# A hybrid attention and state-space layer: ten panels of the input projection with their channels in rows, a new panel order, and other groupings in the state-space part

## The chip, the cores and the metric

The kernel runs on one core of a Trainium2 chip. The metric is the device time of one execution in microseconds. Three runs of the kernel before took 601.91 to 602.18 us, their median 602.09 us.

## What is computed

One layer of a decoder over 256 tokens of width 1024, in float32. One combined input projection feeds an attention mixer and a Mamba-2 mixer that run side by side; their gated sum, a SwiGLU feed-forward block and a gated embedding term follow.

```python
h = rms_norm(x, ln1_g)                       # 256 x 1024
q, k, v, z, xbc, dt_raw, gate_a, gate_b = split(h @ w_in)
qh, kh = rms_norm per head of q, k           # 16 heads of 64
y_a = causal_attention(qh, kh, v) @ w_o_attn # one block of 256 tokens
xbc = silu(causal_depthwise_conv(xbc, conv_w, conv_b))   # 3072 channels, 4 taps
xs, bm, cm = split(xbc)                      # 2048, 4 groups x 128, 4 groups x 128
dt = softplus(dt_raw + dt_bias); a = -exp(a_log) * dt    # 32 heads
# two chunks of 128 tokens; per group of 8 heads:
y = ((cm @ bm.T) * exp(segsum(a))) @ (xs * dt)           # inside a chunk
y += exp(cumsum(a)) * (cm @ state of the chunk before)   # carried state
y = (y + d_skip * xs) * silu(z)
y_b = rms_norm(y, per group of 512, ssm_norm_g) @ w_o_ssm
x += (sigmoid(gate_a) * y_a + sigmoid(gate_b) * y_b) @ w_out
x += (silu(g) * u) @ w_down                  # g, u = rms_norm(x, ln2_g) @ w_gate_up
x += (p @ w_ple_proj) * sigmoid(rms_norm(x, ln3_g) @ w_ple_gate)
```

## The kernel before

**Products in three parts.** Every weight and every activation is split into two float32r numbers, a high one and the rest, and a product a·w is formed as ah·wh + ah·wl + al·wh (`Panel.step`, L355). A chunk of 4 x 128 rows by 512 columns of weights comes in two loads of 512 KB on SyncE's queue into a `raw` tile; `split_w` (L260) makes `wh` by a cast on ScalarE (its line in the trace is L151, the helper `act`) and `wl` by a subtraction on VectorE (L263). `w_tiles` (L255) holds 4 `raw`, 3 `wh` and 6 `wl` tiles of [128, 2, 512]. The activations `h_act` are the transposed inputs times the gain, split, without the row's 1/rms; the 1/rms (`rstd1`, from `x_stats`, L389) comes in when a result leaves PSUM.

**Panels.** `PANELS` (L34) lists the blocks of 512 columns of the input projection in the order of the work; `yb` stands for a block of the state-space output projection. A `Panel` (L333) takes two `psg` banks (tile `g`, four in all), one for each 128 tokens: the activations of 128 tokens are the stationary side, 512 columns of weights move, so the tokens come to stand in the rows. Eight blocks of 128 rows, two token halves and three parts are 48 products of 512 columns. The main loop (L903 to L910) goes through the list, opens a panel, runs its products and starts its evacuation.

**Evacuation.** q and k (`evac_qk`, L556) are normed on VectorE, with a power on GpSimd for each token half, then transposed. v and the gates `ga`, `gb` leave by a copy or a Tanh on ScalarE. xbc (`evac_xbc`, L499) and z (`evac_z`, L533) need their channels in the rows: two evacuations with the scale rstd1 on ScalarE into `s2` tiles, four groups of transposes on TensorE (L192) into `psb` banks (tile `pb`, four), two groups for each half of the panel, then for xbc a ScalarE multiplication by the last tap and three shifted multiply-adds on VectorE (L520), and a SiLU by Tanh.

**The state-space part.** `dt_task` (L416) forms dt by 16 products of 256 columns, then a chain of small operations, and `e0`, `e1`, the decays to the end and from the start of a chunk. `ssm_task` (L608) goes through four groups of eight heads, each in two runs of four heads (`units`, L716). Of a group, `prep` (L645) transposes xs and multiplies it by dt; of a run, `decay_rows` (L628) fills rows on GpSimd and by two small loads, `seg` (L669) forms the decay by a product and an Exp and multiplies it with the scores (L676), `out_` (L681) makes eight products with 64 stationary columns, two at a time on the two halves of the array (`halves`). `off` (L697) adds the carried state: one float32 product of 512 columns, a multiplication by e1 with heads in the columns (L705), four transposes and an addition (L713). `ssm_finish` (L734) multiplies with z and splits the result for the output projection.

**What sets the order.** TensorE runs one list: the panel products are chained in program order, and between two of them the `Filler` (L78) puts products of side tasks. It keeps a clock of its own, `fill.now`, which each product moves on; a task yields the time from which it may go on, which is the present time plus a number of `LAG` (L68). So `LAG` and the ranks of the tasks decide after which panel product a transpose or a score stands. ScalarE and VectorE work through their lists in order too; there the compiler's scheduler sets the order by four priorities (`w` for weight splits, `ev` for evacuations, `bg` for side tasks, `mm`), of which `w` goes first. Tiles come from pools, so that a new tile waits until the last reader of the one in its place is done.

## Time and profile before

| | |
|---|---|
| median of three runs | 602.09 us |
| the profiled execution: span from its first to its last instruction | 600.7 us |
| TensorE busy (matmuls) | 593.9 us, 99%, 2965 instructions |
| weight loads into TensorE | 484.6 us, 81% |
| VectorE busy | 424.1 us, 71% |
| ScalarE busy | 338.6 us, 56% |
| GpSimd busy | 38.7 us, 6% |
| mean granted TensorE clock | 1.000 |
| moved by DMA | 103.88 MB, 173 GB/s |

The profile is of one execution. A matmul's record runs longer than its share of the engine's time, because matmuls overlap in the pipeline: the 1508 records of products from `wh` have a mean of 395 ns, while their starts lie some 227 ns apart. What a product costs is therefore read from the distance of starts in the timeline, or from a stretch of the chain divided by its count. In rows of the trace `g` is a bank of a panel, `pb` a bank of a side task, `s` any working tile.

### The profile page before, as it was taken

Reading aid. Unit: us, or ns where it says so; the run is one execution under the profiler, and the core shown is the slowest. Engines: PE = TensorE matmul, PEld = TensorE weight load, DVE = VectorE, ACT = ScalarE, POOL = GpSimd, SP = SyncE. Lnnn points to the kernel's source line nnn. Section 1 sums busy time; section 2 is a strip of 40 time slices with the busy share of each in tenths; the row PEclk is TensorE's granted clock in tenths of the full one; section 3 lists DMA queues with packets and bytes.
Section 4 is the critical chain, followed back from the end, with each engine's and each line's share of the span. In section 5 each row is a group of like instructions: output and inputs, shape, how many; then the busy total and the mean of one; then the engine's idle time right before and its main releaser. Section 6 shows DMA issues by size and latency. Waiting matters only on the chain.

```text
span 600.7 us, 8147 instructions
## 1 busy us (share of the span) xinstructions
PE 593.9 (99%) x2965; PEld 484.6 (81%) x2965; DVE 424.1 (71%) x668; ACT 338.6 (56%) x513; POOL 38.7 (6%) x47
## 2 busy tenths in 40 slices
PE   8999999999999999999999999999999999999997
PEld 7888888787777878887787788888888888888886
DVE  5689999978997765677875475756756666646465
ACT  6766666556775545576646444755544544445353
POOL 2000103412010011101000000000000000000000
PEclk9999999999999999999999999999999999999999
DMA  8945644533444445555544475556565555555641
GB/s 278 323 152 175 210 142 142 174 131 117 140 127 149 143 150 170 187 166 160 162 161 164 139 232 188 185 165 208 163 200 188 161 201 187 190 188 182 201 141 70
DMA packets 31192, 103.88 MB, mean 173 GB/s; under 512 B 3568, under 2 KB 4912, under 8 KB 31152
## 3 DMA queue, kind: packets, MB, share of 16 engines
q1 hardware_dynamic: 31152, 103.36, 53.3%
q8 instruction: 23, 0.38, 0.3%
q14 instruction: 17, 0.14, 0.1%
HBM read 102.23 MB, written 1.05 MB: 172 GB/s over the span
## 4 chain that ended last, share of the span: by engine, by line
PE 96%; DVE 1%; DMA 1%; ACT 0%; SPq 0%; issue 0%; ACTq 0%
PE g L170 85%; PE pb L170 6%; PE pb L192 5%; DMA raw<-in_head 1%; SPq L248 0%; DVE s L750 0%; ACT wh L151 0%; DVE s L658 0%; ACT s L151 0%; DVE wl L263 0%; DVE s L785 0%; DVE s L663 0%; DVE s L742 0%; DVE s L1063 0%; DVE s L1064 0%
## 5 line engine op out<-in xcount | busy, mean ns | idle before, releaser
L170 PE MATMUL g<-wh,s 128*128 128x512 f32 (+1 forms) x1508 | 486.7, 395 | 0.6 <-ACT wh L151 0.6
L170 PEld LDWEIGHTS g<-wh,s 128*128 128x128 f32 x1508 | 282.7, 189 | 59.6 <-issue 1.8
L263 DVE TENSOR_TENSOR wl<-raw,wh 128x1024 fp32r<-128x1024 f32 (+2 forms) x193 | 230.4, 1196 | 129.6 <-ACT wh L151 127.0
L151 ACT ACTIVATE wh<-raw 128x1024 fp32r<-128x1024 f32 (+2 forms) x193 | 199.9, 1038 | 177.7 <-PE g L170 149.8
L170 PE MATMUL g<-wl,s 128*128 128x512 f32 (+1 forms) x754 | 294.2, 392 | 0.0
L170 PEld LDWEIGHTS g<-wl,s 128*128 128x128 f32 x754 | 142.1, 189 | 27.8 <-issue 1.0
L151 ACT ACTIVATE s<-pb 128x512 f32<-128x512 f32 (+4 forms) x64 | 33.6, 544 | 30.4 <-PE pb L192 16.1
L192 PEld LDWEIGHTS pb<-ident,s 128*128 128x128 f32 x302 | 37.9, 140 | 11.4 <-issue 0.9
L192 PE MATMUL pb<-ident,s 128*128 128x128 f32 x302 | 47.1, 272 | 0.0
L151 ACT ACTIVATE s<-g,rstd 128x512 f32<-128x512 f32 (+1 forms) x50 | 28.5, 583 | 20.5 <-PE g L170 18.7
L520 DVE SCALAR_TENSOR_TENSOR s<-pb,vecs,s 128x255 f32<-128x255 f32 (+2 forms) x72 | 32.0, 475 | 1.4 <-ACT s L151 1.2
L170 PE MATMUL pb<-s,s 128*64 128x128 f32 (+6 forms) x328 | 32.6, 304 | 0.4 <-ACT s L151 0.4
L151 ACT ACTIVATE s<-pb,vecs 128x256 f32<-128x256 f32 (+2 forms) x48 | 25.9, 550 | 11.1 <-PE pb L192 5.0
L170 PEld LDWEIGHTS pb<-s,s 128*64 128x64 f32 (+2 forms) x328 | 23.1, 154 | 9.9 <-issue 4.7
L381 POOL TENSOR_TENSOR rstd<-tiny,mhalf 128x2 f32<-128x2 f32 x3 | 2.3, 762 | 315.2 <-DVE tiny L380 295.3
L151 ACT ACTIVATE s<-s 128x512 f32<-128x512 f32 (+3 forms) x24 | 19.0, 792 | 4.3 <-DVE s L978 4.0
L571 POOL TENSOR_TENSOR tiny<-tiny,mhalf 128x8 f32<-128x8 f32 x8 | 16.0, 1995 | 73.2 <-DVE tiny L569 73.2
L635 POOL TENSOR_SCALAR_AFFINE_SELECT rr<-a_h 128x512 fp32r<-128x512 f32 x16 | 13.6, 860 | 100.2 <-PE pb L170 61.7
L151 ACT ACTIVATE s<-s,tiny 128x128 f32<-128x128 f32 (+1 forms) x32 | 14.2, 444 | 6.5 <-DVE tiny L788 6.5
L1022 DVE SCALAR_TENSOR_TENSOR s<-g,rstd,s 128x256 f32<-128x256 f32 x22 | 10.6, 481 | 7.5 <-ACT s L151 7.5
L676 DVE TENSOR_TENSOR s<-s,s 128x512 f32<-128x512 f32 x16 | 11.9, 748 | 0.3 <-ACT s L151 0.3
L1023 DVE SCALAR_TENSOR_TENSOR s<-g,rstd,s 128x256 f32<-128x256 f32 x22 | 10.7, 484 | 0.7
(120 smaller groups left out, 235.2 us busy)
## 6 DMA issues: line engine op xcount, KB each, us to landing
raw<-in_w_big SPq DMA_DIRECT2D x176, 512.0 KB
raw<-in_head SPq DMA_DIRECT2D x4, 512.0 KB
s<-in_xk SPq DMA_DIRECT2D x4, 512.0 KB
raw<-in_head SPq DMA_DIRECT2D x7, 256.0 KB
raw<-in_w_pp SPq DMA_DIRECT2D x2, 512.0 KB
raw<-in_w_dn SPq DMA_DIRECT2D x2, 512.0 KB
out<-s SPq DMA_DIRECT2D x3, 256.0 KB
xraw<-in_head SPq DMA_DIRECT2D x2, 256.0 KB
```

Of the source, the lines that this page charges most:

```text
L151: return nc.scalar.activation(o, i, f, **kw)
L170: ins = nc.tensor.matmul(o, lhsT, rhs, start=start, stop=stop).ins
L192: queue(nc.tensor.transpose(o, i, ident[: i.shape[0], : i.shape[0]]).ins, False)
L263: nc.vector.tensor_sub(wl, raw, wh.bitcast(F32))
L381: nc.gpsimd.tensor_tensor(dst, t, mhalf[:, : ss.shape[-1]], op=ALU.pow)
L520: stt(cc[:, sft:], pu[:, j, : T - sft], cw[3 - sft], cc[:, sft:], op0=ALU.mult, op1=ALU.add)
L571: nc.gpsimd.tensor_tensor(f, ms, mhalf, op=ALU.pow)
L635: nc.gpsimd.affine_select(r, bcast(a_h[:, c, h0 : h0 + 4].bitcast(F32), P), pattern=[[0, 4], [1, P]], compare_op=ALU.is_ge, fill=0.0, base ...
L676: nc.vector.tensor_tensor(m, m, cbm[:, g, c].unsqueeze(1).to_broadcast([P, 4, P]), op=ALU.mult)
L1022: stt(t[:, tt], pan.ps[tt][:, :T], r, t[:, tt], op0=ALU.mult, op1=ALU.mult)
L1023: stt(t[:, tt], pan.ps[tt][:, T:], r, t[:, tt], op0=ALU.mult, op1=ALU.mult)
```

## The change

**Panel order.** v, q and k come first, then a gate, all six xbc panels, all four z panels, and the rest; before, the six xbc panels came first. `LAG` has other numbers.

**Normed rows.** A new task `norm_task` spreads rstd1 over the partitions by a float32 product with a matrix of ones, multiplies the transposed input by it in place on VectorE, and splits the result times the gain again into high and low parts `hn`. x_stats now stands ahead of dt_task and norm_task. Gates use the normed rows, so their Tanh has the scale 0.5.

**xbc** goes through a class `Rows`: 128 columns of weights are stationary, and the moving side is a row of 512 columns, the high and low parts of the normed input side by side. With `wh` all 512 move, with `wl` the 256 of the high part. A panel takes all four `psg` banks (tile `gr`), one for each 128 channels; 32 products of 512 and 32 of 256 columns are a panel. After a block's last product ScalarE copies the bank, VectorE adds its halves, and the convolution follows: there are no transposes.

**z** goes through a class `Narrow`: the same with three products of 256 columns for each block, two blocks in a bank (tile `gn`), 96 products a panel. Tanh and multiplication take the bank directly.

**dt** is formed from the normed input by eight float32 products on four quarters of the array's columns; the quarters are summed by VectorE. The decay e1 is made with heads in rows, stored to DRAM and loaded twice, 512 KB each, as `e1c`, spread over the rows of each head.

**The state-space part.** `out_` takes all eight heads of a group, 16 products, in one run; the decay rows of a group's both runs are made together, a group ahead. `off` forms the carried state as four float32 products of 128 columns with the channels in rows, so that a multiplication by `e1c` and an addition finish it. `evac_qk` does the power for both token halves at once.

**Buffers.** `s4` 26 to 22, `raw` 4 to 5, `wh` 3 to 4.

On TensorE, at the last block of one xbc panel and the first of the next, the order changes as follows. Before, with transposes of the panel before (`pb`, from its copies `s2`) between the products of a panel, in bank `g_88` (`s4_7` to `s4_10` are activations):

```order
L170 MATMUL g_89_548<-wh_94_556,s4_9_114 128x512
L170 MATMUL g_88_547<-wh_99_600,s4_8_113 128x512
L192 MATMUL pb_97_580<-ident_83,s2_87_545 128x128
L192 MATMUL pb_97_580<-ident_83,s2_86_543 128x128
L192 MATMUL pb_97_580<-ident_83,s2_87_545 128x128
L170 MATMUL g_88_547<-wl_100_601,s4_8_113 128x512
L170 MATMUL g_88_547<-wh_99_600,s4_10_115 128x512
L192 MATMUL pb_104_614<-ident_83,s2_86_543 128x128
L192 MATMUL pb_104_614<-ident_83,s2_87_545 128x128
L192 MATMUL pb_104_614<-ident_83,s2_86_543 128x128
L192 MATMUL pb_104_614<-ident_83,s2_87_545 128x128
L170 MATMUL g_88_547<-wh_99_600,s4_8_113 128x512
```

Now, from the fourth bank of one panel (`gr_208`) to the first of the next (`gr_229`, in the place of `gr_205`; `s4_38` and `s4_35` are normed rows):

```order
L170 MATMUL gr_208_1062<-s4_38_209,wh_219_1116 128x512
L170 MATMUL gr_208_1062<-s4_38_209,wl_220_1117 128x256
L170 MATMUL gr_208_1062<-s4_38_209,wh_219_1116 128x512
L170 MATMUL gr_208_1062<-s4_38_209,wl_220_1117 128x256
L170 MATMUL gr_229_1197<-s4_35_206,wh_234_1202 128x512
L170 MATMUL gr_229_1197<-s4_35_206,wl_235_1203 128x256
L170 MATMUL gr_229_1197<-s4_35_206,wh_234_1202 128x512
L170 MATMUL gr_229_1197<-s4_35_206,wl_235_1203 128x256
L170 MATMUL gr_230_1198<-s4_35_206,wh_234_1202 128x512
```

The transposes are gone, products of two widths alternate, and the next panel needs the bank of a block that ended three blocks earlier.

On ScalarE at the end of an xbc panel stood before the evacuations of two banks (`s2_106`, `s2_107` from `g_88`, `g_89`) among weight casts (`wh` from `raw`) and convolutions (`s4_96` from `pb`):

```order
L151 ACTIVATE s2_106_651<-g_88_547,rstd1_202 128x512
L151 ACTIVATE wh_114_664<-raw_113_663 128x1024
L151 ACTIVATE s4_85_528<-s4_75_468 128x1024
L151 ACTIVATE s4_96_579<-pb_97_580,vecs_106 128x256
L151 ACTIVATE s4_96_579<-pb_104_614,vecs_106 128x256
L151 ACTIVATE wh_119_708<-raw_118_707 128x1024
L151 ACTIVATE s2_107_653<-g_89_548,rstd1_202 128x512
L151 ACTIVATE wh_122_714<-raw_121_713 128x1024
```

Now stand there the evacuations of the four banks `gr_205` to `gr_208` (second boundary; `s4_150` from `pb` are casts of k's transposes, `s4_175` a Tanh):

```order
L151 ACTIVATE wh_240_1248<-raw_239_1247 128x1024
L151 ACTIVATE s2_223_1155<-gr_205_1059 128x512
L151 ACTIVATE s4_150_794<-pb_222_1148,vecs_108 128x4x128
L151 ACTIVATE s2_224_1166<-gr_206_1060 128x512
L151 ACTIVATE s4_175_902<-s4_176_903 128x1024
L151 ACTIVATE s2_225_1177<-gr_207_1061 128x512
L151 ACTIVATE wh_243_1254<-raw_242_1253 128x1024
L151 ACTIVATE s2_226_1188<-gr_208_1062 128x512
```

The evacuation of the fourth bank stands behind a weight cast into a `wh` tile whose place the panel's last products still read.

On VectorE in the state-space part, before, an `out_` run of four heads is two rows of L694, `off` is L705 and L713, and between two such operations stand weight splits (`wl`), the multiplication of z (L551) and that of the decay (L676):

```order
L676 TENSOR_TENSOR s2_281_1419<-s2_281_1419,s4_128_753 128x512
L583 SCALAR_TENSOR_TENSOR s4_221_1183<-pb_282_1425,vecs_106,s4_220_1182 128x4x128
L263 TENSOR_TENSOR wl_305_1532<-raw_303_1530,wh_304_1531 128x1024
L551 SCALAR_TENSOR_TENSOR s4_283_1435<-s4_283_1435,pb_284_1436 128x512
L694 SCALAR_TENSOR_TENSOR s4_132_771<-s4_132_771,dsk_206,pb_285_1452 128x256
L694 SCALAR_TENSOR_TENSOR s4_132_771<-s4_132_771,dsk_206,pb_286_1453 128x256
L551 SCALAR_TENSOR_TENSOR s4_283_1435<-s4_283_1435,pb_297_1488 128x512
L739 TENSOR_TENSOR s4_85_528<-s4_85_528,s4_283_1435 128x1024
L263 TENSOR_TENSOR wl_335_1666<-raw_333_1664,wh_334_1665 128x1024
```

Now the same place reads (L768 is `out_`, L780 and L781 are `off`, L733 and L738 `prep`, L622 z, L809 the product with z):

```order
L768 SCALAR_TENSOR_TENSOR s4_227_1195<-s4_227_1195,dsk_211,pb_499_2725 128x256 x2
L768 SCALAR_TENSOR_TENSOR s4_227_1195<-s4_227_1195,dsk_211,pb_500_2726 128x256 x2
L780 TENSOR_TENSOR s2_502_2764<-pb_501_2759,e1c_216 128x512
L733 TENSOR_TENSOR s4_503_2779<-pb_504_2780,dth_210 128x512
L781 TENSOR_TENSOR s4_227_1195<-s4_227_1195,s2_502_2764 128x4x128
L622 SCALAR_TENSOR_TENSOR s4_473_2595<-s4_473_2595,gn_474_2596 128x512
L738 TENSOR_TENSOR s2_505_2786<-s4_503_2779,e0_214 128x512
L733 TENSOR_TENSOR s4_503_2779<-pb_506_2802,dth_210 128x512
L809 TENSOR_TENSOR s4_227_1195<-s4_227_1195,s4_389_2115 128x1024
L265 TENSOR_TENSOR wl_528_2882<-raw_526_2880,wh_527_2881 128x1024
```

A group's operations now stand in one run between two weight splits.

The diff, cut to its core:

```diff

```diff
+    ('gb', 0, 9248),
+    ('xbc', 5, 7680),
     ('xbc', 4, 7168),
-    ('xbc', 0, 5120),
-    ('xbc', 5, 7680),
...
-        return sb.tile([P] + shape, dt, tag="s4", bufs=26, name=nm("s4"))
+        return sb.tile([P] + shape, dt, tag="s4", bufs=22, name=nm("s4"))
...
-        return (sb.tile([P, 2, 512], F32, tag="raw", bufs=4, name=nm("raw")),
-                sb.tile([P, 2, 512], F32R, tag="wh", bufs=3, name=nm("wh")),
+        return (sb.tile([P, 2, 512], F32, tag="raw", bufs=5, name=nm("raw")),
+                sb.tile([P, 2, 512], F32R, tag="wh", bufs=4, name=nm("wh")),
...
+    class Rows:
+        def __init__(self):
+            self.ps = [psg.tile([P, 512], F32, tag="g", name=nm("gr")) for _ in range(4)]
+        def add_all(self, acts, after):
+            for k0 in range(0, 8, 2):
+                if k0 % 4 == 0:
+                    parts = next_chunk()
+                for b in range(4):
+                    cs = slice(b * P, b * P + P)
+                    for k in (k0, k0 + 1):
+                        (wh, wl), hl_ = parts[k % 4], acts[k]
+                        with prio("mm"):
+                            mm(self.ps[b], wh[:, cs], hl_, k == 0, False, main=True)
+                            mm(self.ps[b][:, :T], wl[:, cs], hl_[:, :T], False, k == 7, main=True)
+                        fill.now += 26.0
+                    fill.step()
+                    if k0 == 6:
+                        after(b, self.ps[b])
+    class Narrow:
...
+                    for k in (k0, k0 + 1):
+                        (wh, wl), (ah, al) = parts[k % 4], acts[k]
+                        for n, (w, a) in enumerate(((wh, ah), (wh, al), (wl, ah))):
+                            with prio("mm"):
+                                mm(o, w[:, cs], a, k == 0 and n == 0 and b % 2 == 0, k == 7 and n == 2 and b % 2 == 1, main=True)
+                            fill.now += 13.0
...
+    def norm_task():
+        yield fill.now + LAG["norm"]
+        with prio("bg"):
+            dg = s2([2, P])
+            for tt in range(2):
+                act(dg[:, tt], ident, scale=rstd1[:, tt : tt + 1])
+            pr = pb([512])
+            mm(pr[:, :T], ones_m, dg.rearrange("p a t -> p (a t)"), True, True)
+            rbc = s2([2, T])
+            for j in range(2):
+                act(rbc[:, j], pr[:, :T])
+        for k in range(0, 8, 2):
+            with prio("bg"):
+                if k:
+                    nc.vector.tensor_mul(xraw[k // 2], xraw[k // 2], rbc)
...
+            yield fill.now + LAG["norm.x"]
+            with prio("bg"):
+                for j in range(k, k + 2):
+                    g = g1[:, j : j + 1]
+                    act(hn_act[j][0], xr_of(j), scale=g)
+                    stt(hn_act[j][1], xr_of(j), g, hn_act[j][0].bitcast(F32), op0=ALU.mult, op1=ALU.subtract)
+            yield fill.now + LAG["norm.k"]
+        done.add("norm")
...
-            for k in range(8):
-                ah, al = h_act[k]
-
-                if k:
-                    mm(pd[:32, :T], wd[:, k - 1, 0], h_act[k - 1][1], False, False)
-                if k == 7:
-                    mm(pd[:32, :T], wd[:, k, 0], al, False, False)
-                mm(pd[:64, :T], wd[:, k].rearrange("p a h -> p (a h)"), ah, k == 0, k == 7)
+            halves(
+                (pd[32 * (k % 4) : 32 * (k % 4) + 32, :T], wdt[:, k], xr_of(k), k < 4, k >= 4)
+                for k in range(8))
             dtT = s2([T])
-            act(dtT[:64], pd[:64, :T])
+            act(dtT, pd[:, :T])
...
+            nc.sync.dma_start(e1d, e1t[:32])
+            for a in range(2):
+                nc.sync.dma_start(e1c[rows_of[a]], e1d.rearrange("(j a) l -> a j l", a=2)[a : a + 1].to_broadcast([64, 16, P]))
...
+    def rows_xbc(i):
+        def after(b, ps):
+            ct = 4 * i + b
+            cw = [v[:, V_CW + 4 * ct + m : V_CW + 4 * ct + m + 1] for m in range(4)]
+            with prio("ev"):
+                e = s2([512])
+                act(e, ps)
+            with prio("bg"):
+                nc.vector.tensor_add(u[:, b], e[:, :T], e[:, T:])
+                cc = c[:, b]
+                act(cc, u[:, b], AF.Identity, scale=cw[3], bias=v[:, V_CB + ct : V_CB + ct + 1])
+                for sft in (1, 2, 3):
+                    stt(cc[:, sft:], u[:, b, : T - sft], cw[3 - sft], cc[:, sft:], op0=ALU.mult, op1=ALU.add)
...
+        def after(jj, ps):
+            zz = zs[:, 2 * jj : 2 * jj + 2]
+            with prio("ev"):
+                act(zz, ps, AF.Tanh, scale=0.5)
+                stt(zz, zz, 1.0, ps, op0=ALU.add, op1=ALU.mult)
...
-                yds = [pb([2, P]) for _ in range(2)]
+                yds = [pb([2, 2, P]) for _ in range(2)]
 
                 halves(
-                    (yds[j][rows_of[hf], c], xdt[:, c, (2 * qd + j) * P + 64 * hf : (2 * qd + j) * P + 64 * hf + 64],
-                     ms[g, qd, c][:, 2 * j + hf], True, True)
-                    for j in range(2) for c in range(2) for hf in range(2))
-                for j in range(2):
-                    i = 2 * qd + j
-                    stt(y[:, i], xs[:, i], dsk[:, 4 * g + i : 4 * g + i + 1], yds[j].rearrange("p c l -> p (c l)"), op0=ALU.mult, op1=ALU.add)
+                    (yds[i // 2][rows_of[hf], i % 2, c], xdt[:, c, i * P + 64 * hf : i * P + 64 * hf + 64],
+                     ms[g, i // 2, c][:, 2 * (i % 2) + hf], True, True)
+                    for i in range(4) for c in range(2) for hf in range(2))
...
-                po = pb([512])
-                mm(po, cb[:, g], xe, True, True)
-                yo = s2([512])
-                nc.vector.tensor_tensor(
-                    yo.rearrange("p (h d) -> p h d", d=64), po.rearrange("p (h d) -> p h d", d=64),
-                    bcast(e1[:, 8 * g : 8 * g + 8], 64), op=ALU.mult)
-            yield fill.now + LAG["off"]
-            with prio("bg"):
-                pt_ = pb([4, P])
+                po = pb([4, P])
                 for i in range(4):
-                    transpose(pt_[:, i], yo[:, i * P : i * P + P])
-                nc.vector.tensor_add(y[:, :, P:T], y[:, :, P:T], pt_)
+                    mm(po[:, i], xe[:, i * P : i * P + P], cb[:, g], True, True)
+                yo = s2([4, P])
+                nc.vector.tensor_mul(yo, po, e1c[:, 4 * g : 4 * g + 4])
+                nc.vector.tensor_add(y[:, :, P:T], y[:, :, P:T], yo)
...
+        for qd in range(2):
+            yield from seg(0, qd)
+        for g in range(4):
+            if g < 3:
+                for qd in range(2):
+                    decay_rows(g + 1, qd)
+            yield max(ms[g, 1] + LAG["out"], st[g][2] + LAG["out.xdt"])
+            yield from out_(g)
+            yield from off(g)
+            fill.spawn(ssm_finish(g), 2, LAG["finish"])
+            if g < 3:
+                yield from prep(g + 1)
+                for qd in range(2):
+                    yield from seg(g + 1, qd)
+                    yield fill.now + LAG["seg.next"]
...
+            pan.add(next_chunk(), (hn_act if norm else h_act)[4 * hf : 4 * hf + 4], last=hf == 1)
```

More of the change, by code (lines that the diff above doesn't have):

```diff
@@ L34 @@
 PANELS = [
+    ('v', 0, 2048),
+    ('v', 1, 2560),
+    ('q', 0, 0),
+    ('q', 1, 512),
+    ('k', 1, 1536),
+    ('k', 0, 1024),
+    ('gb', 0, 9248),
+    ('xbc', 5, 7680),
     ('xbc', 4, 7168),
-    ('xbc', 0, 5120),
-    ('xbc', 5, 7680),
     ('xbc', 1, 5632),
@@ L556, in evac_qk, with rows_z, end @@
+    def rows_z(i):
+        zs = s4([4, T])
+        def after(jj, ps):
[3 more added lines that the diff above has]
+                stt(zz, zz, 1.0, ps, op0=ALU.add, op1=ALU.mult)
+        def end():
+            yield fill.now + LAG["z.end"]
+            zsT[i] = zs
+        return after, end
     def evac_qk(kind, i, pan):
@@ L679, in seg, with out_ @@
             ms[g, qd] = fill.now
[L681 removed]
+        def out_(g):
             xdt = st[g][0]
```

207 lines of the change are left out of this document (94 added, 113 removed).

## The prediction

> **What bounds the kernel now.** I read the page first, then the stretches of equal length, the chain of waits, and the timeline of single engines. In the page TensorE (PE) is busy for 593.9 of 600.7 us, and the chain that ended last lies on it for 96%:
>
> ```profile
> span 600.7 us, 8147 instructions
> PE 593.9 (99%) x2965; PEld 484.6 (81%) x2965; DVE 424.1 (71%) x668; ACT 338.6 (56%) x513; POOL 38.7 (6%) x47
> ...
> PEclk9999999999999999999999999999999999999999
> ...
> PE 96%; DVE 1%; DMA 1%; ACT 0%; SPq 0%; issue 0%; ACTq 0%
> ```
>
> Busy is not yet paced, so I looked for gaps. The stretches (span, then PE, weight loads, VectorE, ScalarE, GpSimd busy, clock, DMA share, GB/s) show none outside the third, although VectorE is at 28.2 and 28.6 of 30 us there:
>
> ```profile
> 30.00:60.00 30.00, 30.00 (x146) 24.43 (x145) 26.47 (x59) 20.12 (x30) 0.00 (x0) 1.00 0.53 164
> 60.00:90.00 30.00, 30.00 (x151) 25.14 (x150) 28.24 (x56) 19.27 (x32) 3.09 (x5) 1.00 0.54 176
> 90.00:120.00 30.00, 29.63 (x156) 23.77 (x155) 28.63 (x49) 17.77 (x25) 11.67 (x9) 1.00 0.49 158
> ```
>
> The timeline of PE names two gaps, one behind an Exp on ScalarE, one behind a sum on VectorE:
>
> ```profile
> 108.33 1.15 PE L170 MATMUL pb<-s,s 128*64 128x128 f32 x16 [0.37 <-ACT s L151]
> ...
> 170.89 0.61 PE L170 MATMUL pb<-ones,s 128*128 128x1 f32 x4 [0.34 <-DVE s L744]
> ```
>
> So the time is a list of matmuls that follow each other without a break, at full clock, and the change is priced by what it takes from that list and by the gaps it opens. The chain (start, us, what) gives the pace of three kinds of matmul:
>
> ```profile
> 129.09 1.31 PE pb L192 x12
> ...
> 520.22 27.69 PE g L170 x122
> ...
> 594.90 1.45 PE pb L170 x12
> ```
>
> That is 27.69/122 = 0.227 us for a product that moves 512 columns, 1.45/12 = 0.121 for one of 256 (the closing products into a pb bank), 1.31/12 = 0.109 for a transpose.
>
> **The change part by part.** Counts are from the two programs as built, prices from these rows and the following PE timeline:
>
> ```profile
> 30.20 0.39 PE L170 MATMUL g<-wh,s 128*128 128x512 f32 x1
> 30.43 0.60 PE L192 MATMUL pb<-ident,s 128*128 128x128 f32 x4
> 30.79 0.48 PE L170 MATMUL g<-wh,s 128*128 128x512 f32 x1
> 31.10 0.40 PE L170 MATMUL g<-wl,s 128*128 128x512 f32 x1
> ...
> 27.86 2.04 PE L170 MATMUL pb<-s,s 128*64 128x256 f32 x16
> 29.73 0.40 PE L170 MATMUL g<-wh,s 128*128 128x512 f32 x1
> ...
> 78.88 1.47 PE L170 MATMUL pb<-s,s 128*128 128x256 f32 x8
> 80.11 0.48 PE L170 MATMUL g<-wh,s 128*128 128x512 f32 x1
> 80.42 0.40 PE L170 MATMUL g<-wl,s 128*128 128x512 f32 x1
> ...
> 213.01 1.09 PE L170 MATMUL pb<-s,s 128*64 128x128 f32 x16
> 214.03 0.50 PE L170 MATMUL g<-wh,s 128*128 128x512 f32 x1
> ...
> 214.83 1.02 PE L170 MATMUL pb<-s,s 128*128 128x512 f32 x2
> 215.29 0.79 PE L170 MATMUL g<-wh,s 128*128 128x512 f32 x1
> 215.92 0.40 PE L170 MATMUL g<-wl,s 128*128 128x512 f32 x1
> ```
>
> - *Transposes.* Gone are 8 in each of six xbc and four z panels and 16 of the carried state: 96, in 24 groups of four. From 30.43 to 31.10 lie a group and one product: 0.67 - 0.227 = 0.44 us a group. 24 x 0.44 = **-10.6**.
> - *Products of the ten panels.* 480 of 512 columns go; 192 of 512 and 576 of 256 come. (192 - 480) x 0.227 + 576 x 0.121 = -65.4 + 69.7 = **+4.3**. If a 256 cost half of a 512, it would be 0; the closing row is the same shape with its own weight load, so I take 4.3. The Trainium skill (TensorE: Matmul & The Clock Gate, section Back-to-back issue gap) gives an isolated warm gap of N/2.4 + 2.5 ns, 109 and 216 ns; by that the exchange would come to an estimated +0.7. The trace has 121 and 227, and the sum stays with it.
> - *Carried state (off).* Of each group one float32 product of 512 becomes four of 128. Before: 215.92 - 214.83 - 0.227 = 0.86. The row at 78.88 holds two float32 products of 256 columns and two of 128 in 80.42 - 78.88 - 0.227 = 1.31, so 0.44 and 0.22: four of 128 are 0.87. **0**.
> - *dt.* Sixteen products took 29.73 - 27.86 = 1.87. Now eight float32 ones of 256 columns stand on quarters of the array: 0.9 if four run at once, 3.5 if none do. The nearest row is the half-array one at 213.01: eight float32 products of 128 in 1.02 where one after another they would take 1.76. Two at a time bring the factor 0.6; for four I take 0.43, so 1.5: **-0.4**.
> - *Normed rows.* One float32 product more (0.44): **+0.4**. Its 16 casts and subtractions and five multiplications run beside the q and k panels, in the stretch 30 to 60 us, from which the convolutions leave. If that cover failed, the first row-wise panel would wait for them; it comes some 50 us after the first cast can start.
> - *Runs of eight heads.* The same 64 products in four groups for eight: fewer changes between full and half array, but more of attention's score groups are now split by a panel product. Between -0.6 and +0.6: **0**.
>
> Sum on PE: -10.6 + 4.3 - 0.4 + 0.4 = **-6.3 us**. The two gaps shown (0.37 + 0.34) lie at places that no longer exist in this form: **-0.7**.
>
> What is added in waits has to be worked out from the order on ScalarE (ACT) and VectorE. Their prices:
>
> ```profile
> 106.75 1.05 ACT L151 ACTIVATE wh<-raw 128x1024 fp32r<-128x1024 f32 x1
> 107.69 1.07 ACT L151 ACTIVATE s<-pb 128x512 f32<-128x512 f32 x2
> ...
> L151 ACT ACTIVATE s<-pb 128x512 f32<-128x512 f32 x32 | 18.7, 592 | 12.4 <-PE pb L192 8.1 <-PE pb L170 4.3
> L151 ACT ACTIVATE s<-g,rstd 128x512 f32<-128x512 f32 x27 | 17.8, 682 | 11.0 <-PE g L170 9.3 <-PE pb L170 1.8
> ...
> L263 DVE TENSOR_TENSOR wl<-raw,wh 128x1024 fp32r<-128x1024 f32 x184 | 224.7, 1223 | 126.4 <-ACT wh L151 123.9
> L520 DVE SCALAR_TENSOR_TENSOR s<-pb,vecs,s 128x253 f32<-128x253 f32 x24 | 11.3, 475 | 0.1
> L572 DVE TENSOR_TENSOR s<-g,tiny 128x512 f32<-128x512 f32 x8 | 5.5, 685 | 1.1 <-POOL tiny L571 1.1
> L744 DVE TENSOR_TENSOR s<-s 128x256 f32<-128x256 f32 x4 | 1.7, 414 | 0.0
> ```
>
> - *All four banks for one xbc panel.* Before, a panel held two of four g banks, and its evacuation had the whole next panel. Now the next panel returns to a bank after three other blocks: 3 x 2 x (0.227 + 0.121) = 2.09 us. The fourth block's evacuation stands on ACT behind a weight split that waits for the panel's very last product (the wh buffer). A product's record outlasts its pace by 0.17 (0.40 - 0.227); a split keeps ACT for 0.94 (106.75 to 107.69), the evacuation takes 0.59: 1.70, so 0.39 is spare and the plain boundary costs nothing. At the first two boundaries more stands there (two casts of k's transposes, a Tanh of 1024 elements); counted through in ACT's order they miss by some 0.2 and 0.5 us. At the entrance (gate panel to first xbc panel) block two comes 0.70 us after the gate panel (two products of each width) and dt's four small products, some 0.35 as I estimate (four transposes are 0.44); the bank's Tanh (0.68) waits behind a split: 0.17 + 0.94 + 0.68 = 1.8 against 1.05: 0.75. Together **+1.5**.
> - *VectorE in the SSM stage.* From z's third panel to the first ga panel its order holds 22 operations of 1024 elements, 51 of 512, 36 of about 256 and 49 small ones: 22 x 1.223 + 51 x 0.685 + 36 x 0.475 = 78.9 us, some 90 with the small ones. PE has 121 x 0.227 + 190 x 0.121 = 50.5 us of panel products there and 20 to 25 of others. Four wh buffers, of 2.7 us each beside other work, let VectorE run some 13 us ahead. Its records overlap (two stretches above: 28 us busy for operations that sum to over 30), so 90 is about 85 us against 84 to 88: it just fits. I add **+1.0**, and keep 0 and 5 as ends.
> - *Covered.* The four new adds of a panel stand on VectorE, not on PE: an xbc panel asks VectorE for 4 x 1.223 + 4 x 0.414 + 12 x 0.475 + 1.2 = 13.5 us by records against 11.1 on PE, but the backlog is spent on convolutions that SSM needs only after the last xbc panel, and the splits go ahead. The spread of the decay (a store and two 512 KB loads on SyncE's queue) stands before weight loads whose panel begins two panels, 22 us, later; weights use half of the DMA (0.54, 0.49). Were that cover gone, it would cost one landing, a few us, once. The joint power for q and k releases banks later, but a bank has 10.9 us. More raw and wh tiles find no gap to fill.
>
> Sum: 600.7 - 6.3 - 0.7 + 1.5 + 1.0 = 596.2 us of span. Between span and median lie 602.09 - 600.7 = 1.4 us of start and end, unchanged: **597.6 us**.
>
> **The rivals.**
> - *No new gaps.* The order keeps ACT and VectorE ahead everywhere, as it does now; dt at 0.9. 600.7 - 6.3 - 0.7 - 0.6 + 1.4 = 594.5. For it: today's order has only 0.7 us of gaps at 95% VectorE. Against: the bank arithmetic above. Chance 0.20 (below 595.5).
> - *The bank return costs at every boundary.* If a semaphore's way and ACT's other work eat the 0.39 spare, each of five boundaries loses 0.5 to 1.0, and PE's start of z the same: 597.6 + 2 to 4 = 600 to 601.5. Chance 0.12.
> - *VectorE becomes the bound of the SSM stage, and the kernel slower.* Place: z's third panel to first ga panel. VectorE works in order; it waits there for score products, Exps and out products that PE reaches later. It fits only if it idles less than 3 us; each further us is a us of PE. From some 9 us of idling on the gain is gone; with 12: 600.7 - 6.3 - 0.7 + 1.5 + 12 + 1.4 = 608.6. For it: heads in runs of eight put more work between waits, and this stage is denser than any of today's. Against: PE lost only 0.37 us at 28.6 of 30. Chance 0.10.
> - *The weight loads set the pace.* The ten panels now load weights 768 times for 480. Were a 256 held to the mean of a load, 0.189, the exchange would cost 576 x 0.068 = 39 us more: 637.
>
> ```profile
> L170 PEld LDWEIGHTS g<-wh,s 128*128 128x128 f32 x1508 | 282.7, 189 | 59.6 <-issue 1.8
> ```
>
>   The closing 0.121 row, one load per product, speaks against it: 0.02. The same section of the Trainium skill gives a sustained 81 ns at 128 columns and 131 at 512, load included, so an estimated 98 at 256 and +19 us for the exchange; the 0.227 of this trace disagrees with it.
>
> **How the numbers follow.** A difference of 0.2% (1.2 us) is about what a measurement of this kernel can tell from none: faster ends at 600.9. Forecast with its own bounds (595.5 to 600): 0.56; no gaps 0.20; banks 0.12, half of it under 600.9; VectorE 0.10; loads 0.02. Faster 0.56 + 0.20 + 0.06 = 0.82, same 0.06, slower 0.12. The range runs from 593.0 (no gaps, a 256 a little under its row) to 601.5.
>
> **What would show it.** Right: transposes down from 303 to 207, 256-column products of gr and gn at 0.12 us, PE's gaps in single figures of tenths at the first products of the gr panels. Wrong: 256-column products above 0.13; gr products waiting for ACT at each panel; PE waiting for wl in the SSM stage; a gap before the first gr panel that names the normed rows.

## The result, and the profile after

The changed kernel took 595.53 us (median of four runs, 595.08 to 597.27) against 602.13 us for the kernel before: a ratio of 0.9898, 95% interval 0.9884 to 0.9912, so it is faster by 6.6 us. The forecast was 597.6 us, the range 593.0 to 601.5. The profiled execution took 595.48 us, its span 593.8 us, 6.9 us less than before.

The page of the changed kernel, engines and instructions:

```profile
span 593.8 us, 8655 instructions
...
PE 585.2 (99%) x3183; PEld 493.4 (83%) x3183; DVE 439.8 (74%) x703; ACT 340.9 (57%) x528; POOL 38.7 (7%) x44
```

TensorE is still the bound, with 8.7 us less of busy time in more instructions. The waits of TensorE (engine and line, what it waited for, us in total, times, longest):

```profile
PE pb L205 <- DVE ones L209: 1.1, 1, 1.1
PE pb L170 <- ACT s L151: 0.9, 1, 0.9
PE gr L170 <- ACT s L151: 0.9, 2, 0.7
PE g L170 <- ACT wh L151: 0.7, 1, 0.7
PE g L170 <- DVE s L647: 0.6, 1, 0.6
PE g L170 <- DVE wl L265: 0.3, 1, 0.3
```

The first, the fourth and the last lie in the first 18 us, where the weights arrive. Four waits in the middle are new. The timeline of TensorE shows their places (start, us, what; in brackets the wait before it), with dt's products at 60.06 among them:

```profile
50.08 0.39 PE L170 MATMUL g<-wh,s 128*128 128x512 f32 x1
51.02 0.47 PE L170 MATMUL g<-wh,s 128*128 128x512 f32 x1 [0.56 <-DVE s L647]
...
60.06 0.40 PE L170 MATMUL pb<-x,s 128*32 128x256 f32 x1
...
61.06 0.50 PE L170 MATMUL g<-wh,s 128*128 128x512 f32 x1
...
88.04 0.22 PE L170 MATMUL pb<-le_r,a_l 128*32 128x128 f32 x1
88.95 0.50 PE L170 MATMUL gr<-s,wh 128*128 128x512 f32 x1 [0.68 <-ACT s L151]
...
114.75 0.28 PE L170 MATMUL gr<-s,wl 128*128 128x256 f32 x1
115.21 0.50 PE L170 MATMUL gr<-s,wh 128*128 128x512 f32 x1 [0.17 <-ACT s L151]
...
195.89 0.82 PE L192 MATMUL pb<-ident,s 128*128 128x128 f32 x6
197.56 2.41 PE L170 MATMUL pb<-s,s 128*64 128x256 f32 x28 [0.86 <-ACT s L151]
```

The wait at 88.95 is the entrance of the xbc panels, that at 115.21 their second boundary; the other two were not in the forecast. The transposes (all records of L192 on TensorE) went from 303 to 207, as the forecast's sign had it. On ScalarE, at the entrance, the gate's second Tanh stands behind a weight split, as the order said:

```profile
87.35 1.06 ACT L151 ACTIVATE wh<-raw 128x1024 fp32r<-128x1024 f32 x1 [0.30 <-PE g L170]
88.32 0.58 ACT L151 ACTIVATE s<-g 128x512 f32<-128x512 f32 x1
```

The chain gives the pace of the new products, and the stretches show VectorE (third busy time) in the xbc panels (first row), z's panels and the larger part of the state-space part:

```profile
115.21 21.77 PE gr L170 x124
...
170.46 4.54 PE gn L170 x38
```

```profile
120.00:150.00 30.00, 30.00 (x178) 25.97 (x178) 29.97 (x65) 20.93 (x33) 0.00 (x0) 1.00 0.55 176
150.00:180.00 30.00, 30.00 (x225) 27.28 (x224) 25.67 (x66) 23.81 (x53) 0.00 (x0) 1.00 0.49 158
180.00:210.00 30.00, 29.14 (x256) 26.78 (x256) 28.58 (x71) 21.83 (x55) 2.20 (x2) 1.00 0.33 101
210.00:240.00 30.00, 30.00 (x282) 27.12 (x281) 28.14 (x53) 17.74 (x35) 8.59 (x7) 1.00 0.34 105
240.00:270.00 30.00, 30.00 (x171) 25.17 (x170) 28.66 (x44) 20.61 (x31) 3.65 (x5) 1.00 0.41 133
```

A pair of 512 and 256 columns takes 2 x 21.77/124 = 0.351 us, a product of 256 in z 4.54/38 = 0.119. VectorE is busy for 28 to 29 of 30 us over the last 90 us, and for 29.97 of 30 in the xbc panels of the first row, where the forecast had counted more records on VectorE than TensorE takes. TensorE waits for it nowhere there.

### The profile page after: what moved, and what is told of

Its sections match the earlier page's. It is cut to its first block, busy times and chain, and to the rows that moved or that the text cites. A ratio compares the mean times of both kernels' runs of the same rounds, so it can differ in the third digit from the quotient of the medians.

```text
span 593.8 us, 8655 instructions
## 1 busy us (share of the span) xinstructions
PE 585.2 (99%) x3183; PEld 493.4 (83%) x3183; DVE 439.8 (74%) x703; ACT 340.9 (57%) x528; POOL 38.7 (7%) x44
## 3 DMA queue, kind: packets, MB, share of 16 engines
HBM read 103.28 MB, written 1.06 MB: 176 GB/s over the span
## 4 chain that ended last, share of the span: by engine, by line
PE 93%; ACT 2%; DMA 2%; DVE 1%; POOL 1%; issue 1%; SPq 1%; ACTq 0%
PE g L170 64%; PE gr L170 10%; PE gn L170 8%; PE pb L170 6%; PE pb L192 4%; ACT wh L151 1%; DMA raw<-in_head 1%; DMA xraw<-in_head 1%; ACT s L151 1%; POOL tiny L644 1%; DVE wl L265 1%; SPq L250 1%; DVE s L647 0%; DVE tiny L640 0%; DVE tiny L642 0%
## 5 line engine op out<-in xcount | busy, mean ns | idle before, releaser
L170 PE MATMUL g<-wh,s 128*128 128x512 f32 (+1 forms) x1188 | 374.6, 392 | 1.2 <-ACT wh L151 0.7
L265 DVE TENSOR_TENSOR wl<-raw,wh 128x1024 fp32r<-128x1024 f32 (+2 forms) x193 | 231.0, 1200 | 113.4 <-ACT wh L151 111.0
L151 ACT ACTIVATE wh<-raw 128x1024 fp32r<-128x1024 f32 (+2 forms) x193 | 200.1, 1038 | 179.6 <-PE g L170 131.1
L170 PEld LDWEIGHTS g<-wh,s 128*128 128x128 f32 x1188 | 222.5, 188 | 47.1 <-ACT wh L151 1.1
L170 PE MATMUL g<-wl,s 128*128 128x512 f32 (+1 forms) x594 | 230.5, 390 | 0.3 <-DVE wl L265 0.3
L170 PEld LDWEIGHTS g<-wl,s 128*128 128x128 f32 x594 | 111.5, 188 | 22.3 <-DVE wl L265 0.9
L170 PE MATMUL gr<-s,wh 128*128 128x512 f32 x192 | 69.1, 401 | 0.9 <-ACT s L151 0.9
L170 PE MATMUL gr<-s,wl 128*128 128x256 f32 x192 | 54.0, 281 | 0.0
L170 PE MATMUL gn<-s,wh 128*128 128x256 f32 x256 | 49.0, 288 | 0.0
L151 ACT ACTIVATE s<-pb 128x512 f32<-128x512 f32 (+3 forms) x58 | 29.0, 531 | 29.2 <-PE pb L192 16.7
L170 PEld LDWEIGHTS gr<-s,wh 128*128 128x128 f32 x192 | 36.0, 188 | 9.5 <-ACT s L151 1.5
L170 PEld LDWEIGHTS gn<-s,wh 128*128 128x128 f32 x256 | 40.2, 191 | 1.0 <-issue 0.3
L170 PE MATMUL gn<-s,wl 128*128 128x256 f32 x128 | 37.0, 289 | 0.0
L170 PEld LDWEIGHTS gr<-s,wl 128*128 128x128 f32 x192 | 36.3, 189 | 0.3
L192 PE MATMUL pb<-ident,s 128*128 128x128 f32 x206 | 33.0, 273 | 0.0
L170 PE MATMUL pb<-s,s 128*64 128x128 f32 (+5 forms) x336 | 30.9, 295 | 0.9 <-ACT s L151 0.9
L192 PEld LDWEIGHTS pb<-ident,s 128*128 128x128 f32 x206 | 25.7, 140 | 6.0
L170 PEld LDWEIGHTS pb<-s,s 128*64 128x64 f32 (+2 forms) x336 | 24.4, 158 | 6.7 <-issue 2.2
L170 PEld LDWEIGHTS gn<-s,wl 128*128 128x128 f32 x128 | 24.4, 191 | 0.4
L151 ACT ACTIVATE s<-s 128x512 f32<-128x512 f32 (+2 forms) x23 | 18.6, 810 | 6.8 <-DVE s L1061 4.0
```

The source lines that it names most:

```text
L151: return nc.scalar.activation(o, i, f, **kw)
L170: ins = nc.tensor.matmul(o, lhsT, rhs, start=start, stop=stop).ins
L192: queue(nc.tensor.transpose(o, i, ident[: i.shape[0], : i.shape[0]]).ins, False)
L265: nc.vector.tensor_sub(wl, raw, wh.bitcast(F32))
```

## The experiments

All are changes of the changed kernel, and their results stand beside its 595.53 us. The theory was the forecast's: TensorE's list sets the time, VectorE just keeps up with it in the state-space stage, and the banks' return opens small gaps. The rivals were that VectorE decides, or that the gaps are worth something else than they last. Runs of one kernel lie up to 2 us apart, and much of that is the arrival of the first weights: the same panel product, ahead of nearly all that the edits touch, begins at 18.11 us in the trace of the changed kernel, at 17.04 in `e9_ev_first` and at 19.24 in `e11_two_gaps`. So sizes under 1 us are read from the traces, where needed from the first xbc product to the end, which leaves the arrival out. `e10` to `e13` ran on another chip, where the kernel before took 602.45 us for 602.0 to 602.2; a few tenths between the two groups mean nothing.

**z again with tokens in rows** (`e1_z_panels`):

```diff
-    "dt.end": 1000, "xbc": 3513, "xbc.t": 2655, "xbc.end": 16932, "z": 9234, "z.t": 0, "z.end": 2000,
+    "dt.end": 1000, "xbc": 3513, "xbc.t": 2655, "xbc.end": 16932, "z": 7477, "z.t": 2878, "z.end": 2196,
...
+    evac = {"z": lambda k, i, p: evac_z(i, p), "q": evac_qk, "k": evac_qk,
...
-        if kind in ("xbc", "z"):
+        if kind == "xbc":
...
-        norm = kind in ("ga", "gb")
+        norm = kind in ("ga", "gb", "z")
```

> The changed kernel, but z's four panels again with tokens in rows (48 products of 512 columns from the normed rows), copied by ScalarE and transposed. By the sum: a panel gains 96 x 0.121 - 48 x 0.227 = 0.72 us of products and pays two transpose groups, 0.88: +0.16 a panel, +0.6 us in all, 596.2 us, hardly apart from the changed kernel's 595.5. Rival, that the row form of z carries the gain because the copies and transposes also hold up ScalarE and the banks: over 2 us more, 597.5 or above.

607.92 us, +12.4: far above both. The timeline of TensorE between two z panels:

```profile
206.38 2.41 PE L170 MATMUL pb<-s,s 128*64 128x256 f32 x28
...
210.07 0.44 PE L192 MATMUL pb<-ident,s 128*128 128x128 f32 x2 [0.69 <-ACT s L151]
...
214.74 0.66 PE L192 MATMUL pb<-ident,s 128*128 128x128 f32 x4 [1.35 <-DVE tiny L878]
216.39 1.97 PE L170 MATMUL pb<-rr,gt_r 128*128 128x512 f32 x3 [1.00 <-issue]
218.66 0.77 PE L170 MATMUL pb<-rr,gt_r 128*128 128x512 f32 x1 [0.30 <-ACT s L151]
...
220.36 0.78 PE L170 MATMUL g<-wh,s 128*128 128x512 f32 x1
```

From 206.38 to 220.36, for 14 us, no panel product runs: scores, value products, transposes and decay products stand in one row, and several wait for ScalarE or VectorE with nothing put between. The granted clock is 0.50 from 217 to 223 us, behind these waits, of which the longest is 1.35. So this run does not measure the form of z; it measures a row of side tasks that has lost its cover. The edit also gives z's three numbers in `LAG` back the values of the kernel before, while all other numbers stay. Whether the row comes of the form or of these numbers was not tried, and what the form alone is worth stays open.

**xbc again with tokens in rows** (`e2_xbc_panels`), with the evacuation of the kernel before, without its scale:

```diff
-    "dt.end": 1000, "xbc": 3513, "xbc.t": 2655, "xbc.end": 16932, "z": 9234, "z.t": 0, "z.end": 2000,
+    "dt.end": 1000, "xbc": 3815, "xbc.t": 1507, "xbc.end": 7967, "z": 9234, "z.t": 0, "z.end": 2000,
...
+    evac = {"xbc": lambda k, i, p: evac_xbc(i, p), "q": evac_qk, "k": evac_qk,
...
-        if kind in ("xbc", "z"):
+        if kind == "z":
...
-        norm = kind in ("ga", "gb")
+        norm = kind in ("ga", "gb", "xbc")
```

> The changed kernel, but xbc's six panels again with tokens in rows, copied and transposed. By the sum: a panel pays 0.88 us of transposes and gains 32 x 0.121 - 16 x 0.227 = 0.24 of products: +0.64 a panel, +3.8 in all; the bank waits of the entrance and of the second boundary (0.7 and 0.3) go, so 598.2 us. Rival, that the row form of xbc pays nothing because the banks' return eats it: 595.5 or below.

604.86 us, +9.3. The entrance's wait is gone, but there is a new one, and a clock that falls behind it (waits of TensorE; then stretches with the granted clock in the third column from the right):

```profile
PE pb L192 <- DVE s L657: 3.5, 1, 3.5
```

```profile
202.00:204.00 2.00, 0.02 (x1) 0.02 (x1) 2.00 (x4) 2.00 (x5) 0.00 (x0) 1.00 0.80 252
204.00:206.00 2.00, 2.00 (x16) 1.68 (x16) 2.00 (x4) 0.67 (x2) 0.00 (x0) 0.67 0.06 18
206.00:208.00 2.00, 2.00 (x11) 1.93 (x10) 1.97 (x9) 0.00 (x0) 0.00 (x0) 0.50 0.00 0
```

The profiled run is the fastest of five. By spans it is 601.2 - 593.8 = 7.4 us; 3.5 are this wait, and 2 x 0.33 + 2 x 0.50 = 1.7 the clock missing from 204 to 208. The rest is 2.2 us, or 3.2 if one allows that the panel product of 18.11 us begins at 17.15 here; 2.7 were expected for the form with the banks' waits taken off. This speaks against the rival, that the form pays nothing, but does not show the form alone: L657 is the last operation of the old evacuation, and `xbc.end`, the pause that the filler's clock leaves for it, fell from 16932 to 7967 in the same edit. The wait may belong to that number; that was not tried.

**The carried state in its old form** (`e3_off_old`):

```diff
-                    mm(po[:, i], xe[:, i * P : i * P + P], cb[:, g], True, True)
+                mm(po, cb[:, g], xe, True, True)
...
+                    transpose(pt_[:, i], yo[:, i * P : i * P + P])
```

> The changed kernel, but the carried state again as one float32 product of 512 columns, multiplied with heads in columns and transposed; the spread of the decay through DRAM goes with it. By the prediction's prices: four transpose groups come back, 4 x 0.44 = +1.8 us, products equal, 597.3 us. Rival from the trace of the changed kernel, whose 32 products of 128 columns take 3.5 us for 2.8 before: +1.1, 596.6. If the spread cost something on its queue: less than that, 595.5 or below.

597.54 us, +2.0, nearest to the forecast's +1.8; the spread through DRAM costs nothing that shows. That it fits so closely is partly chance. The wait at 51 us, ahead of all that this edit changes in the state-space part, is missing in this trace. From the first xbc product to the end the changed kernel takes 593.8 - 87.15 = 506.6 us and this one 595.6 - 86.12 = 509.5, 2.8 more. So the new form of the carried state pays at least the price of its transposes, the rival's +1.1 is too small, and what the other 1.0 us is stays open.

**z in the form of xbc** (`e4_z_rows`):

```diff
-                Narrow().add_all(hn_act, after)
+                Rows().add_all(hn_rows, after)
```

> The changed kernel, but z takes the same form as xbc: 32 products of 512 and 32 of 256 columns in four banks, a copy by ScalarE and an addition of the halves by VectorE. TensorE gains 96 x 0.121 - 32 x 0.348 = 0.48 us a panel: if TensorE's list sets the time, 593.6 us. VectorE gets 16 additions of 256 (6.7 us) and ScalarE 16 copies (9.5 us) in the stage where VectorE is busy for 28 to 29 of 30 us: if VectorE is the bound there, as the prediction's rival has it, 598 to 601 us, with TensorE waiting for the low weight tiles.

The edit also lets `rows_z` add the halves and take the Tanh from the sum. 613.5 us, +18. The side is the rival's, the size beyond it, and the releaser another. The largest waits of TensorE, then the last wait for a bank, and the clock one microsecond behind it:

```profile
PE gr L170 <- ACT s L151: 5.3, 5, 1.8
PE pb L192 <- DVE s L871: 4.1, 3, 3.7
PE pb L192 <- DVE s L908: 1.6, 1, 1.6
```

```profile
239.75 0.52 PE L170 MATMUL gr<-s,wh 128*128 128x512 f32 x1 [1.77 <-ACT s L151]
```

```profile
241.00:242.00 1.00, 1.00 (x5) 0.79 (x4) 0.96 (x3) 1.00 (x4) 0.00 (x0) 0.50 0.78 172
```

A shorter list on TensorE made the kernel slower: five waits for a bank's copy and four for attention's operations on VectorE, and for a low weight tile only one of 0.5 us. All waits that the view names come to 15.3 us, for 4.5 in the changed kernel. A second part is the clock: 0.50 from 189 to 199, from 217 to 223 and from 241 to 243 us, a mean of 0.983 for 0.999. That is at most 0.016 x 612 = 10 us of the 18.4 by which the span grew, less where TensorE idles in these stretches.

**The buffers** (`e5_wh3`): `raw` 5 to 4, `wh` 4 to 3.

> The changed kernel with raw back from five to four tiles and wh from four to three. If the fourth wh tile is what lets VectorE run ahead through the state-space stage (the prediction's 13 us of lead), TensorE now waits there for low weight tiles: 1 to 5 us, 596.5 to 600.5 us. Rival, that the buffers find no gap to fill: 595.5 us, within 0.5.

597.46 us, +1.9, and TensorE's waits name the low weight tiles:

```profile
PE g L170 <- DVE wl L265: 1.9, 3, 0.7
```

They lie at 247, 271 and 291 us, in the state-space stage. The fifth `raw` and the fourth `wh` tile, which the run does not part, carry TensorE over that stage; together they do fill a gap.

**More work for VectorE** (`e6_dve_load` five times, `e12_dve_load1` twice):

```diff
+                for _ in range(5):
                     nc.vector.tensor_mul(yo, po, e1c[:, 4 * g : 4 * g + 4])
```

> The changed kernel with the multiplication of the carried state done five times over instead of once in each of the four groups: 16 more VectorE operations of 512 elements, 11.0 us, no change of the result. If VectorE just fits, as the prediction has it (less than 3 us to spare), TensorE loses 6 to 10 us: 601 to 606 us. Rival, that VectorE's busy records hide more room than 11 us because operations overlap and splits run ahead: under 1.5 us more, below 597 us.

> The changed kernel with the multiplication of the carried state done twice in each of the four groups: 4 more VectorE operations of 512 elements, 2.75 us, no change of the result. If VectorE has the 3 us to spare that the prediction gave it: 595.5 to 596 us. If it has nothing to spare, as five multiplications suggest (11.0 us more work, 11.9 us more span): 598 to 599 us.

2.75 us more left 595.73 us (+0.2): they fit. 11.0 us more made it 609.55 us, +14.0, more than was added and above the 601 to 606 that were expected. In this run TensorE waits three times (timeline), and after one of them its clock is halved for 6 us, until 269.9 (stretches):

```profile
237.43 0.50 PE L170 MATMUL g<-wh,s 128*128 128x512 f32 x1 [2.58 <-DVE s L622]
263.62 0.99 PE L170 MATMUL pb<-ones,s 128*128 128x1 f32 x4 [2.87 <-DVE s L815]
291.55 0.58 PE L170 MATMUL pb<-ones,s 128*128 128x1 f32 x4 [2.87 <-DVE s L815]
```

```profile
262.00:264.00 2.00, 0.38 (x2) 0.41 (x3) 2.00 (x6) 2.00 (x5) 0.00 (x0) 0.77 0.79 237
264.00:266.00 2.00, 2.00 (x17) 1.98 (x19) 2.00 (x4) 1.90 (x4) 0.45 (x1) 0.50 0.50 190
...
268.00:269.00 1.00, 1.00 (x4) 0.81 (x3) 0.00 (x0) 0.00 (x0) 0.00 (x0) 0.50 0.35 139
```

The waits are 8.3 us and the halved clock some 3, together nearly the 11.9 us by which the profiled span grew (605.7 for 593.8). So the point from which VectorE decides lies between 2.75 and 11 us of added work; the forecast's 3 us lies within, and beyond that point the clock adds to the waits. One thing is not parted: the repeated operation stands in the chain from the carried state to the output projection, so the runs lengthen this chain as well as VectorE's list.

**The power of q and k in two calls** (`e7_pow_halves`), the form of the kernel before:

```diff
-            nc.gpsimd.tensor_tensor(f.rearrange("p a b -> p (a b)"), ms.rearrange("p a b -> p (a b)"), mhalf, op=ALU.pow)
+                nc.gpsimd.tensor_tensor(f, ms, mhalf[:, :8], op=ALU.pow)
```

> The changed kernel with the power of q and k again in two calls of eight columns, one for each token half, each followed by its multiplication. The gap of 0.56 us that the changed kernel's trace has at 50.7 us, before the first product into a bank that the multiplication of the panel two before releases, goes if the joint power makes it: 594.8 us. Rival, that GpSimd's second call comes as late: 595.5 with the gap still there.

594.52 us. The gap moved (first row, timeline of TensorE): the first product into the bank of the first token half has no wait now, and a shorter one stands six products later, at the bank of the second half. Another gap went: at the entrance the second block's products follow dt's small ones at once (second and third row).

```profile
52.55 0.47 PE L170 MATMUL g<-wh,s 128*128 128x512 f32 x1 [0.38 <-DVE s L646]
...
88.19 0.22 PE L170 MATMUL pb<-le_r,a_l 128*32 128x128 f32 x1
88.25 0.45 PE L170 MATMUL gr<-s,wh 128*128 128x512 f32 x1
```

```profile
49.88 1.64 POOL L645 TENSOR_TENSOR tiny<-tiny,mhalf 128x8 f32<-128x8 f32 x1 [2.67 <-DVE tiny L643]
```

The last row is GpSimd's second call: it starts only at 49.88, when VectorE has done the second half's sum, which it did behind a weight split. So the joint call made the wait at the first bank, as expected, and the rival is right for the second: its call comes late.

At the entrance ScalarE ends the gate's second Tanh only at 89.05, behind its split as in the changed kernel, so the second block no longer takes that Tanh's bank: the edit moved the banks around. What the joint power costs net of the new wait is 0.56 - 0.38, some 0.2 us.

**Evacuations at the weights' rank** (`e9_ev_first`):

```diff
             cw = [v[:, V_CW + 4 * ct + m : V_CW + 4 * ct + m + 1] for m in range(4)]
-            with prio("ev"):
+            with prio("w"):
                 e = s2([512])
...
     def evac_gate(kind, n, pan):
-        with prio("ev"):
+        with prio("w"):
```

> The changed kernel with the gates' evacuations given the weight splits' rank, so that on ScalarE the second gate's Tanh at the entrance of the xbc panels stands ahead of the split that it followed. If that split is what holds the bank, as the prediction has it, the gap of 0.68 us at 88.3 us goes: 594.8 us. Rival, that another wait takes its place (the split now comes a Tanh later, and its weights): 595.5 us.

The edit raises the copies of the xbc banks (first part of the diff) as well as the gates' evacuations. 594.15 us. On ScalarE the Tanh now stands ahead of the split, and the gap at the entrance is gone:

```profile
86.28 0.60 ACT L151 ACTIVATE s<-g 128x512 f32<-128x512 f32 x1 [0.30 <-PE g L170]
86.78 1.05 ACT L151 ACTIVATE wh<-raw 128x1024 fp32r<-128x1024 f32 x1
```

The split was the cause, and no new wait is in the list. At the second boundary the higher rank did not change ScalarE's order, and the lost time there stays: the product into the returned bank begins 0.41 us after the one before it, 0.46 in the changed kernel, where 0.12 is the pace. By the medians the edit is worth 1.4 us, but the profiled run has 1.1 of its 1.6 us already before the xbc panels, where the first weights came earlier: from the first xbc product to the end it takes 592.2 - 86.09 = 506.1 us for 506.6. So the edit is worth about 0.5 us, less than the gap; the rest is lost in steps of 0.1 us or so within the xbc panels.

**Gaps taken together** (`e11_two_gaps`: the two edits above; `e10_three_gaps`: with `"val": 1761` in `LAG` raised to 2600 as well; both hold the higher rank of the xbc copies too):

> The changed kernel with two of its gaps taken away, the power of q and k in two calls and the gates' evacuations at the weight splits' rank; side tasks stand where they stood. If the two gains, 1.0 and 1.4 us as measured alone, add up: 593.1 us; by the gaps alone, 0.7 and 0.8: 594.0 us.

> The changed kernel with three of its gaps on TensorE taken away at once: the power of q and k in two calls (0.7 us at 50 us), the gates' evacuations at the weight splits' rank (0.8 us at 88 us), and the pause behind attention's value products in the filler's clock raised from 1761 to 2600, so that six transposes and the value products behind them no longer stand in one row (0.9 us at 197 us). If gaps on TensorE cost what they last, 595.5 - 0.7 - 0.8 - 0.9 = 593.1 us. Rival, that later side work piles up elsewhere on a VectorE without room: 594 us or above, with new gaps behind 200 us.

The two edits gave 593.97 us, ratio to the kernel before 0.9858 (0.9844 to 0.9873). By the medians the gains of 1.0 and 1.4 do not add up, and both edits remove the gap at the entrance. From the first xbc product to the end the traces give 0.8 for `e7_pow_halves`, 0.5 for `e9_ev_first` and 1.3 for both (593.4 - 88.11 = 505.3 us), of which 0.6 comes in z's panels and the state-space part, where side products stand otherwise; so how far they add up is not settled. The median is the lowest here, its interval below that of the changed kernel, and hardly apart from `e9_ev_first` (0.9867, 0.9854 to 0.988). The third edit cost 4.6 us: 598.58. The row of transposes and value products did not part, and waits longer, now for attention's scores on VectorE:

```profile
197.55 1.52 PE L170 MATMUL pb<-s,s 128*64 128x256 f32 x16 [2.18 <-DVE tiny L854]
```

That is 1.3 us of the 4.6; the rest stays open. The profiled run, 597.54 us, is the shortest of six; three of the others, 598.6 to 600.3 us, have a mean granted clock of 0.997 for its 1.000, which over the span is up to 1.8 us.

**dt on one quarter** (`e13_dt_one`):

```diff
-                (pd[32 * (k % 4) : 32 * (k % 4) + 32, :T], wdt[:, k], xr_of(k), k < 4, k >= 4)
+                (pd[:32, :T], wdt[:, k], xr_of(k), k == 0, k == 7)
```

> The changed kernel with dt's eight float32 products all on the first 32 columns of the array, summed in PSUM, in place of four quarters that VectorE sums. If the quarters run side by side, as their 1.0 us for eight products says, the eight now take up to 3.5 us: +2.5, 598.0 us. Rival, that a product with 32 stationary columns is cheap by itself: within 0.5 us of the changed kernel.

596.82 us, +1.3. In the timeline the eight products, sixteen records, begin at 59.56, and the next panel product begins at 63.13:

```profile
59.56 0.62 PE L170 MATMUL pb<-x,s 128*32 128x256 f32 x2
60.02 3.18 PE L170 MATMUL pb<-xraw,s 128*32 128x256 f32 x14
63.13 0.50 PE L170 MATMUL g<-wh,s 128*128 128x512 f32 x1
```

That is 3.57 us for 1.00 on four quarters: the quarters run side by side. The time rose by less than the 2.57, because the wait at the entrance is gone in this order too.

## Why the prediction was right, and where its terms were off

- *Transposes, -10.6, and the ten panels' products, +4.3.* 96 transposes are gone, in two groups of four a panel, as the prediction counts them (the description of the kernel before says four groups). The pace came out as priced: 192 x 0.351 + 384 x 0.119 - 480 x 0.227 = +4.1. So the exchange is not the +0.7 that the rule of the Trainium skill (TensorE: Matmul & The Clock Gate, section Back-to-back issue gap) would have made it. The carried state's form, priced at 1.8 us of transposes, came back as 2.0 by the medians and 2.8 by the traces.
- *dt, -0.4.* Mis-sized: 1.00 us for 1.87 before, -0.9. The forecast took a factor of 0.43 between its bounds; it was the lower bound, four at once.
- *Banks, +1.5.* Right in place and cause at the entrance: forecast at 0.75, it waited 0.68 us, behind the split and the Tanh that the order had named. The second boundary, forecast at 0.5, waited 0.17; the first, 0.2, shows no wait.
- *VectorE, +1.0.* Nothing of it appeared, but the reason for it holds: 2.75 us more work fits, 11.0 do not, and with one `raw` and one `wh` tile less TensorE waits 1.9 us for it. Its working was less sure than it looks: four buffers of 2.7 us are 10.8 us of lead, not 13, so TensorE's side of the comparison was 81 to 86 us against 85, and "it just fits" did not follow from it.
- *Covered at nothing.* The joint power was not: a wait of 0.56 us where the forecast had given a bank 10.9 us. GpSimd's first call takes 3.97 us and begins only when both halves' sums are there:

```profile
46.18 3.97 POOL L644 TENSOR_TENSOR tiny<-tiny,mhalf 128x16 f32<-128x16 f32 x1 [20.08 <-DVE tiny L642]
```

  With two calls the wait at the first half's bank is gone and one of 0.38 stands at the second half's, so the joint call's net price is some 0.2 us. The sentence that more raw and wh tiles find no gap to fill failed: together they are worth 1.9 us.
- *Attention's order.* A wait of 0.86 us at 197.56 that no term had.

The sum on these rows: -10.6 + 4.1 - 0.9 - 0.7 (the two old gaps) + 0.4 (normed rows, as forecast) + 0.85 + 0.56 + 0.86 = -5.4, against 6.9 us less of span. Counted from start to start, as the prices are, the new gaps are 0.85, 0.34, 0.71 and some 0.9 us and the old ones 1.0 together, which makes -5.2. The 1.5 to 1.7 us between are not explained. By `e3_off_old` the carried state may hold 1.0 of them; groups of side products, the runs of eight heads and the arrival of the first weights are other candidates, which the runs don't part. The forecast's -4.5 was right in sign and kind; 1.0 of its miss is the reserve for VectorE, which the buffers of the same change made needless. Some of its closeness is luck: two waits that no term had, 1.4 us, are balanced by the part that is not explained. And 595.53 us lies on the border between the forecast's own bounds and the rival without new gaps (below 595.5), so the time alone does not choose between the two. The waits do: there are new gaps, as the forecast had it, though the banks' are little over half as large.

Two sums of the prediction are off without changing its result. Between span and time lie 1.7 us, not 1.4: the span of 600.7 belongs to a run of 602.45 us, not to the median. And the rival of the banks, 597.6 + 2 to 4, is 599.6 to 601.6.

What the forecast did not see is how narrow its ground is. Taking z's form or xbc's form back, with its three numbers of `LAG`, costs 12.4 and 9.3 us, not the 0.6 and 2.7 of TensorE's list. In the traces side tasks then stand without cover, wait for VectorE or ScalarE, and lose clock; whether the form or the numbers put them there is open. What the runs support is that the gain of 6.6 us is that of the list in this order and with these buffers.

## What to carry to other kernels

When one engine is 99% busy, the sum over its list forecasts an edit well as long as the side work keeps its places between the long products; an edit priced at 0.6 us cost 12.4 here when a run of side tasks lost that cover. Where an evacuation that returns a bank ties with prefetch work on the same engine, look at which stands first: turning one pair around took away a wait of 0.68 us here, of which about 0.5 reached the end. Before taking a difference of medians for the price of an edit, look where in the trace it arises: 1.1 us of one lay ahead of the edit. Test the slack of the second engine by repeating one of its operations: here one repetition in each of four groups was free and four were not.
